# Hymba layer in one Trainium2 core: down products in 3, 4 and 4 pairs, splits in another order, work moved at the stage borders

## The chip, the cores and the metric

One Trainium2 chip, one of its cores. The metric is the device time of one execution of the whole kernel in microseconds (us), lower is better. Five engines work beside each other, each with a queue of its own: TensorE (PE, matmuls; its weight loads are shown as PEld), ScalarE (ACT), VectorE (DVE), GpSimd (POOL) and SyncE (SP, which here issues DMAs).

## The reference

One layer on 512 tokens, with 16 meta tokens put in front (L = 528 columns), width 1024, FFN width 2816, all float32:

```python
h = jnp.concatenate([meta, x], axis=1)
h = h + 0.5 * swiglu_ffn(rms_norm(h, ffn1_norm), ffn1_w_gu, ffn1_w_down)
h = h + hybrid_mixer(rms_norm(h, mix_norm), w_in, conv_w, b_f, ...)   # short conv + attention with forget gates
h = h + 0.5 * swiglu_ffn(rms_norm(h, ffn2_norm), ffn2_w_gu, ffn2_w_down)
return rms_norm(h[:, 16:], final_norm)

def swiglu_ffn(h, w_gu, w_down):
    gate, up = jnp.split(h @ w_gu, 2, axis=-1)
    return (jax.nn.silu(gate) * up) @ w_down
```

## The kernel before

**Layout.** The activations lie transposed: features on the 128 partitions, tokens along the free dimension. The residual stream `hT` has 8 tiles of 128 features. A weight is the stationary operand of a matmul, the activations move past it. Float32 accuracy comes from a split: an operand is cut into a part `hi` (rounded, by a cast on ACT) and a part `lo` (the rest, by a subtraction on DVE), and a product is three matmuls, hi·hi, hi·lo and lo·hi.

**Stages.** FFN1 (528 tokens, in two halves of 264 columns), the mixer, FFN2 (512 tokens, halves of 256), the final norm. At the start of each FFN some gate and up tiles are computed one by one ("classical", with splits on lines L450 and L454), while the forms of the normed input are made. FFN1 splits its last classical weights behind the norm.

**Units.** All else in the FFNs is done in *units*. A unit multiplies a 2x2 block arrangement (two output tiles by two token halves) by a scheme with seven products in place of eight. `gates(f)` and `ups(f)` make two tiles of gate or up over 4 pairs of input tiles; `down(j0, nj, m)` adds `nj` pairs of hidden tiles into two tiles of `hT`. A unit has seven *slots* of 3·nj matmuls each on PE (L522), in this order: p1 (weights `nat`), p4 of the unit before (its weights `s1`), p2 (`nat`), p6 (`s24`), p5 (`s1`), p7 (`s3`), pC (`s24`). p2 may start only when ACT has copied bank B = −A (L535), p7 only after C = −B (L536). A slot of 12 matmuls takes about 1.5 us.

**The weights of a unit** are made in `prep`: SP loads the raw block, two POOL DMAs (L478) add to it in place, DVE makes the sums s2 and s4 (L481, L484), and then each of `nat`, `s24`, `s1`, `s3` is split: `hi` on ACT (L492), one slot later `lo` on DVE (L496). The moving operands are *forms*, which `pair_forms` makes for each pair of tiles (sums on POOL, L379 to L382, hi on ACT, L368, lo on DVE, L369), and they lie in a ring in an arena.

**Order.** Everything is written into numbered slots: `sl.at(t, fn, prio)` puts an instruction beside slot t; within a slot lower `prio` stands first. Results have 0, forms 2, `prep` 3. The engines work through their queues in that order. So a DVE instruction that waits (for the end of a product, say) holds up all that stands behind it on DVE. The results of a unit at slot b on DVE are, for ups: b+3 `times(0,0)`, b+6 `c22` (L581 and L577), b+7 `c12` (L585 and L577), b+9 `times(1,0)` (L577), which reads the bank that p4 ended one slot before; for downs the adds into `hT` (L604, L607, L608) at the same places.

**FFN1's downs** are done in four rounds of 3, 3, 2 and 3 pairs, each of 4 units; in the last round `fin` makes the mixer's operand (L275, L280) and the squares (L289 on ACT, L290 on POOL) for each tile of `hT` as it is done.

Of the kernel before, what the change touches and what calls it, by code (L numbers as in the profile page):

```python
# [14 lines left out]
P = 128  # L15
# [148 lines left out]
def layer(ctx, tc, x, meta, n1, gu1, dn1, nm, w_in, conv_w, b_f, g_conv, g_attn, w_out, n2, gu2, dn2, nf, out):  # L164
# [174 lines left out]
    class Ffn:  # L339
# [31 lines left out]
        def pair_forms(self, r, s0, s1, t0, t1, soon=True):  # L371

            h, ts = self.h, {}
            d, e = (0, 3) if soon else (1, 4)

            def sums():
                t = ts["t"] = self.pool.tile([P, 4, h], F32, name="ts")
                b11, b12, b21, b22 = (self.half(s(), i) for s in (s0, s1) for i in range(2))
                nc.gpsimd.tensor_sub(t[:, 0], b11, b12)  # L379
                nc.gpsimd.tensor_add(t[:, 1], t[:, 0], b22)  # L380
                nc.gpsimd.tensor_sub(t[:, 2], b12, b22)
                nc.gpsimd.tensor_sub(t[:, 3], b21, t[:, 1])  # L382

            self.split_forms(r, F_B11, F_B11 + 1, lambda: self.half(s0(), 0), t0 + d)
            self.sl.at(t1, sums)
            self.split_forms(r, F_B21, F_B22 + 1, lambda: s1()[:, :2 * h].rearrange("p (a c) -> p a c", a=2), t1 + d)
            self.split_forms(r, F_T1, F_T4 + 1, lambda: ts["t"], t1 + e)

        def x_pair(self, j, t):
# [11 lines left out]
            self.pair_forms(self.xform(j), lambda: xs[0], lambda: xs[1], t + 1, t + 1)  # L401

        def hidden_pair(self, j, t0, t1, soon=False):
            self.pair_forms(self.hform(j), lambda: self.hd[2 * j], lambda: self.hd[2 * j + 1], t0, t1, soon)
# [55 lines left out]
        def prep(self, b, mat, c0, j0, nj):  # L460
# [47 lines left out]
        def products(self, nj, rhs, w):  # L508
# [86 lines left out]
        def down(self, j0, nj, m):  # L595
# [3 lines left out]
            b, q, A, B, C, E = self.products(nj, lambda j: self.hform(j0 + j), w)  # L599
# [17 lines left out]

    with tc.tile_pool(name="ps1", bufs=3, space=PSUM) as ps1, tc.tile_pool(name="ps1s", bufs=2, space=PSUM) as ps1s:
# [5 lines left out]
        with tc.tile_pool(name="xin", bufs=1) as xin:  # L624
# [50 lines left out]
            with tc.manual_schedule(engines={mybir.EngineType.PE, mybir.EngineType.Activation, mybir.EngineType.DVE}):  # L675
# [29 lines left out]
                for j in range(3):  # L705
                    t = t528("raw")
                    accs[j].each(lambda ps, g: nc.scalar.copy(g(t), ps))
                    raws_f.append(t)
                h, lo = split2(ssum, L)
                a3, _ = new1()  # L710
                mm(a3, W.take(3), range(4), xh, xl, last=False)
                sms = [ps1s.tile([P, 512], F32, name="sm") for _ in range(2)]
                sa = Acc(sms, L)
                row_sums(sa, h, lo)
                mm(a3, W.take(3), range(4, ND), xh, xl, first=False)
                row_rstd(sa)
                t = t528("raw")
                a3.each(lambda ps, g: nc.scalar.copy(g(t), ps))
                raws_f.append(t)
            gp = ps1s.tile([P, 512], F32, name="sm")  # L720
            nc.tensor.transpose(gp[:, :36], gt, ident[:36, :36])
            nc.vector.tensor_copy(gains[:, 8:], gp[:, :36])
            nc.vector.tensor_scalar(ghalf, gains[:, :24], -0.5, None, ALU.mult)
# [13 lines left out]
    with tc.tile_pool(name="ffn1", bufs=1, reuse_waits="tile") as pool, tc.manual_schedule(engines=ENGINES):  # L737
# [4 lines left out]
        ring = lambda j: 0 if j == 10 else RING + (j + 3) % 4 * 14 * 264  # L742
# [60 lines left out]
    with ExitStack() as mix:  # L803
# [459 lines left out]
```

## Time and profile before

| | |
|---|---|
| median of 3 runs | 1000.1 us (998.0 to 1001.9) |
| the profiled execution | 1000.34 us, its span 998.6 us, so 1.7 us lie around the span |
| PE busy | 951.8 us, 95% of the span |
| DVE, ACT, POOL busy | 780.3 us (78%), 586.1 us (59%), 350.9 us (35%) |
| mean granted clock of TensorE | 0.988 of full |

Busy time of PE includes matmuls at the lower clock, so idle time is not all that PE loses. In rows of the trace "idle before <-X" names what ended the idle time; "128x1024" is partitions by elements.

### The profile page before, as it was taken

To read this page: it belongs to the slowest core of one execution; us is meant where nothing else is said; L and a number is where in the kernel's file an instruction comes from. 1 tells how busy PE (TensorE), PEld (TensorE's weight loads), DVE (VectorE), ACT (ScalarE), POOL (GpSimd) and SP (SyncE) were. 2 spreads that over 40 slices of the span, in tenths; PEclk is the share of its full clock that TensorE was granted. 3 is DMA by queue.
4 is the path that set the end of the run, shared out by engine and by line. 5 is a ranking of instruction groups with operands and counts; after the bars stand their busy time and mean duration, and the time that the engine had idled before them with its cause. 6 is when DMAs were issued, how large, how long until landed. Compare 5 with 4: busy or idle time off the path is not lost.

```text
span 998.6 us, 17874 instructions
## 1 busy us (share of the span) xinstructions
PE 951.8 (95%) x7022; PEld 907.8 (91%) x7022; DVE 780.3 (78%) x1260; ACT 586.1 (59%) x1044; POOL 350.9 (35%) x323
## 2 busy tenths in 40 slices
PE   9898999999999998999999999999999999999995
PEld 8798999999999887989899888778999999999984
DVE  5688887888788887786767657788897988788655
ACT  5544655665666564785656565545655665576444
POOL 4247533553444564100000000365533653444302
PEclk9999999999999999999999999999999999999997
DMA  6236488668784571542222221257589668787612
GB/s 193 64 107 138 100 174 181 134 128 183 164 156 100 116 141 45 130 107 64 64 78 65 77 64 43 79 137 163 108 171 188 133 132 183 172 153 170 130 29 85
DMA packets 176261, 121.01 MB, mean 121 GB/s; under 512 B 5845, under 2 KB 175617, under 8 KB 176177
## 3 DMA queue, kind: packets, MB, share of 16 engines
q1 hardware_dynamic: 117024, 90.42, 29.9%
q0 software_dynamic: 59008, 28.93, 23.8%
q8 instruction: 55, 0.90, 0.4%
q10 hardware_dynamic: 144, 0.52, 0.1%
q14 instruction: 30, 0.24, 0.1%
HBM read 117.69 MB, written 2.10 MB: 120 GB/s over the span
## 4 chain that ended last, share of the span: by engine, by line
PE 73%; DVE 16%; ACT 5%; issue 4%; POOL 1%; DMA 1%; SPq 0%; ACTq 0%; DVEq 0%
PE bank L522 47%; PE bank L318 19%; DVE w_lo L496 4%; DVE arena L369 3%; PE bank L1055 2%; DVE hT L604 1%; DVE w_lo L454 1%; DVE w_lo L81 1%; PE bank L992 1%; PE bank L1022 1%; ACT arena L275 1%; DVE xn L398 1%; PE acc L318 1%; DVE arena L280 1%; ACT w_hi L492 1%
## 5 line engine op out<-in xcount | busy, mean ns | idle before, releaser
L522 PE MATMUL bank<-arena,w_hi 128*128 128x256 f32 (+1 forms) x3080 | 569.4, 287 | 17.5 <-ACT bank L536 10.0
L522 PEld LDWEIGHTS bank<-arena,w_hi 128*128 128x128 f32 x3080 | 481.7, 191 | 24.1 <-ACT bank L536 14.0
L522 PE MATMUL bank<-arena,w_lo 128*128 128x264 f32 (+1 forms) x1540 | 439.4, 285 | 4.5 <-DVE w_lo L496 4.5
L522 PEld LDWEIGHTS bank<-arena,w_lo 128*128 128x128 f32 x1540 | 294.8, 191 | 6.1 <-DVE w_lo L496 5.9
L318 PE MATMUL bank<-arena,w_hi 128*128 128x264 f32 (+2 forms) x1152 | 247.3, 323 | 3.1 <-ACT w_hi L450 3.1
L492 ACT CAST w_hi<-raw 128x1024 fp32r<-128x1024 f32 (+2 forms) x186 | 176.4, 948 | 125.0 <-DVE raw L484 104.2
L496 DVE TENSOR_TENSOR w_lo<-raw,w_hi 128x1024 fp32r<-128x1024 f32 (+2 forms) x186 | 222.9, 1199 | 31.9 <-ACT w_hi L492 30.2
L318 PEld LDWEIGHTS bank<-arena,w_hi 128*128 128x128 f32 x1152 | 179.6, 191 | 18.9 <-ACT w_hi L450 3.5
L318 PE MATMUL bank<-arena,w_lo 128*128 128x264 f32 (+2 forms) x576 | 155.5, 325 | 5.4 <-DVE w_lo L454 5.3
L318 PEld LDWEIGHTS bank<-arena,w_lo 128*128 128x128 f32 x576 | 96.8, 191 | 15.9 <-DVE w_lo L454 8.4
L478 POOL DMA_DIRECT2D s<-in_ffn_w_gu_dram x34 | 49.7, 1462 | 67.9 <-ACT bank L536 65.9
L81 DVE TENSOR_TENSOR w_lo<-raw,w_hi 128x1024 fp32r<-128x1024 f32 (+2 forms) x53 | 55.3, 1052 | 21.0 <-ACT w_hi L80 20.8
L478 POOL DMA_DIRECT2D raw<-in_ffn_w_gu_dram x34 | 44.1, 1298 | 77.2 <-DMA raw<-in_ffn_w_gu_dram 76.7
L80 ACT CAST w_hi<-raw 128x1024 fp32r<-128x1024 f32 (+3 forms) x54 | 44.1, 829 | 45.2 <-PE bank L318 35.6
L478 POOL DMA_DIRECT2D s<-in_ffn_w_down_dram x28 | 41.2, 1471 | 70.8 <-ACT bank L536 67.3
L604 DVE TENSOR_TENSOR hT<-bank,hT 128x264 f32<-128x264 f32 (+1 forms) x112 | 47.5, 424 | 14.5 <-PE bank L522 14.1
L496 DVE TENSOR_TENSOR w_lo<-s,w_hi 128x512 fp32r<-128x512 f32 (+2 forms) x62 | 46.8, 755 | 0.0
L193 ACT ACTIVATE s<-s 128x256 f32<-128x256 f32 (+3 forms) x42 | 19.4, 461 | 46.5 <-DVE s L561 26.6
L474 ACT COPY s<-raw 128x512 f32<-128x512 f32 (+2 forms) x62 | 35.5, 572 | 17.6 <-DVE w_lo L496 15.2
L369 DVE TENSOR_TENSOR arena<-ts,arena 128x1056 fp32r<-128x1056 f32 (+1 forms) x29 | 35.9, 1237 | 9.4 <-ACT arena L368 9.4
L481 DVE TENSOR_TENSOR raw<-raw 128x512 f32<-128x512 f32 (+2 forms) x62 | 42.0, 677 | 0.8
L478 POOL DMA_DIRECT2D raw<-in_ffn_w_down_dram x28 | 35.4, 1265 | 15.1 <-DMA raw<-in_ffn_w_down_dram 14.5
(231 smaller groups left out, 1170.9 us busy)
## 6 DMA issues: line engine op xcount, KB each, us to landing
raw<-in_ffn_w_gu_dram SPq DMA_DIRECT2D x34, 1024.0 KB, 6.7
raw<-in_ffn_w_down_dram SPq DMA_DIRECT2D x20, 768.0 KB, 4.4
raw<-in_w_in_dram SPq DMA_DIRECT2D x24, 512.0 KB, 4.1
raw<-in_ffn_w_gu_dram POOLq DMA_DIRECT2D x34, 256.0 KB, 4.8
s<-in_ffn_w_gu_dram POOLq DMA_DIRECT2D x34, 256.0 KB, 6.2
raw<-in_ffn_w_gu_dram SPq DMA_DIRECT2D x16, 512.0 KB, 4.0
raw<-in_ffn_w_down_dram SPq DMA_DIRECT2D x4, 1024.0 KB, 5.1
raw<-in_ffn_w_down_dram POOLq DMA_DIRECT2D x20, 192.0 KB, 4.4
```

The costliest lines, as they stand in the source:

```text
L80: nc.scalar.copy(h, src)
L81: nc.vector.tensor_sub(lw, src, h.bitcast(F32))
L318: nc.tensor.matmul(ap, lhsT=wt[:, kw, :], rhs=mt[:, k, c0 - off:c1 - off], start=(first and a == 0 and b == 0), stop=(last and a == len(ks ...
L369: self.sl.at(t + 1, lambda: nc.vector.tensor_sub(lo, src(), hi.bitcast(F32)), 2)
L474: nc.scalar.copy(raw["s3"], raw["all"][:, 0::2, 0])
L478: nc.gpsimd.dma_start(out=t, in_=mat_j[:, i, :, c0 + P:c0 + 2 * P], accum_op=ALU.add)
L481: nc.vector.tensor_add(raw["all"][:, 0::2, 0], raw["all"][:, 0::2, 1], raw["all"][:, 0::2, 0])
L492: nc.scalar.copy(w[nm_][0][:, :m], src(nm_))
L496: nc.vector.tensor_sub(w[nm_][1][:, :m], src(nm_), w[nm_][0][:, :m].bitcast(F32))
L522: nc.tensor.matmul(bank, lhsT=wt[:, idx(j), :], rhs=r[:, form, part], start=(start and i == 0), stop=(i == last), skip_group_check=True)
L604: return lambda: nc.vector.tensor_add(t, ps, t)
L1055: nc.tensor.matmul(oo, lhsT=lt, rhs=rt, start=(a == 0 and n_ == 0), stop=(a == 1 and n_ == len(ops) - 1))
```

## The change

1. **The order of the splits in every unit.** `prep` splits `s1` at slot b and `s24` at b+1; before it was `s24` at b and `s1` at b+1. `nat` and `s3` stay where they were.
2. **FFN1's downs** go in three rounds of 3, 4 and 4 pairs, at other places between the gates and ups: 28 units in FFN1 in place of 32, with the same number of matmuls. The forms of the last hidden pair are made one by one (`last_pair`), their sums on DVE. In the first unit of the last round p5 stands ahead of p2 and p6 (`late`).
3. **Forms at the FFNs' start.** The pairs of the normed input stand 6 slots apart in place of 5, from slot 8 (FFN1) and 5 (FFN2) in place of 9 and 6; a different part of each pair is split early; two hidden pairs move by one or two slots.
4. **FFN1's start.** The transposes of the gains stand ahead of the norm's sums, and two weights (gate and up of tile 2) are loaded and split ahead of the classical products that use them.
5. **FFN2's end.** The loads of the last two weight rows are issued 12 and 11 slots earlier, and their splits two slots earlier.
6. Some addresses of the mixer's operands in the arena change.

```diff
-        def pair_forms(self, r, s0, s1, t0, t1, soon=True):
+        def pair_forms(self, r, s0, s1, t0, t1, e, d=0):
-            d, e = (0, 3) if soon else (1, 4)
...
-            self.pair_forms(self.xform(j), lambda: xs[0], lambda: xs[1], t + 1, t + 1)
+            self.pair_forms(self.xform(j), lambda: xs[0], lambda: xs[1], t + 1, t + 1, 4)
...
+        def last_pair(self, j, b):
...
+            split(F_B11, 1, lambda: src(0, 0), b + 3)
+            split(F_B22, 1, lambda: src(1, 1), b + 6)
+            sl.at(b + 7, sums, 0)
+            split(F_T1, 3, lambda: v["t"][:, :3], b + 7)
+            sl.at(b + 9, lambda: nc.vector.tensor_sub(v["t"][:, 3], src(1, 0), v["t"][:, 1]), 0)
+            split(F_B21, 1, lambda: src(1, 0), b + 9)
+            split(F_T4, 1, lambda: v["t"][:, 3], b + 9)
...
-            for nm_, t in (("nat", b - 4), ("s24", b), ("s1", b + 1), ("s3", b + 2)):
+            for nm_, t in (("nat", b - 4), ("s1", b), ("s24", b + 1), ("s3", b + 2)):
                 sl.at(t, lambda nm_=nm_: hi(nm_), 3)
                 sl.at(t + 1, lambda nm_=nm_: lo(nm_), 3)
...
+            for p in (p5, p2, p6) if late else (p2, p6, p5):
+                sl.slot(p)
...
+            wts2 = [split_raw2(0)]
             row_rstd(sa)
             table(SILU_SET)
+            out_of(a3)
+            wts2.append(split_raw2(1))
...
-            F.x_pair(j, 9 + 5 * j)
+            F.x_pair(j, 8 + 6 * j)
...
         g_units(range(8, 14))
+        F.gates(14)
         for m in range(0, ND, 2):
-            F.down(3, 3, m)
-        g_units(range(14, NF))
+            F.down(3, 4, m)
+        t = F.ups(14)
+        F.hidden_pair(7, t, t)
+        g_units(range(16, NF - 2))
+        F.gates(NF - 2)
+        F.ups(NF - 2)
+        F.last_pair(NF // 2 - 1, len(sl.pe) - 7)
         for m in range(0, ND, 2):
-            F.down(6, 2, m)
-        for m in range(0, ND, 2):
-            for i, t in enumerate(F.down(8, 3, m)):
+            for i, t in enumerate(F.down(7, 4, m, m == 0)):
...
-                F.x_pair(j, 6 + 5 * j)
-            F.hidden_pair(0, n0 - 5, n0 - 5, True)
-            F.hidden_pair(1, n0 + 1, n0 + 1, True)
+                F.x_pair(j, 5 + 6 * j)
+            F.hidden_pair(0, n0 - 3, n0 - 3, True)
+            F.hidden_pair(1, n0 + 2, n0 + 2, True)
...
-                sl.at(n - 10 + 6 * i, W.load, 4)
-                sl.at(n - 4 + 3 * i, lambda: W.split(False), 4)
+                sl.at(n - 22 + 7 * i, W.load, 4)
+                sl.at(n - 6 + 3 * i, lambda: W.split(False), 4)
```

How this moves instructions in the built programs is shown at three places. **First place:** DVE's queue in a gates unit that follows an ups unit (FFN2), before the change. `w_lo_8803` is the lo part of `s24`, `w_lo_8820` that of `s1`, and the `L577` between them is `times(1,0)` of the ups, which reads the bank of p4:

```order
L577 SCALAR_TENSOR_TENSOR s_8603<-v_8782,s_8603 128x256
L496 TENSOR_TENSOR w_lo_8803<-raw_8538,w_hi_8802 128x1024
L577 SCALAR_TENSOR_TENSOR s_8604<-bank_7071,s_8604 128x256
L496 TENSOR_TENSOR w_lo_8820<-raw_8538,w_hi_8819 128x1024
L496 TENSOR_TENSOR w_lo_8837<-s3_8615,w_hi_8836 128x512
```

The same place in the changed program, where `w_lo_8682` belongs to `s1` and `w_lo_8699` to `s24`:

```order
L604 SCALAR_TENSOR_TENSOR s_8482<-v_8661,s_8482 128x256
L521 TENSOR_TENSOR w_lo_8682<-raw_8417,w_hi_8681 128x1024
L604 SCALAR_TENSOR_TENSOR s_8483<-bank_6950,s_8483 128x256
L521 TENSOR_TENSOR w_lo_8699<-raw_8417,w_hi_8698 128x1024
L521 TENSOR_TENSOR w_lo_8716<-s3_8494,w_hi_8715 128x512
```

The lo part of `s24`, which p6 reads, now stands behind the instruction that waits for p4, where the lo part of `s1` stood, which p5 reads one slot later.

**Second place:** ACT's queue at the start of FFN2, where its classical products begin, before the change; `xn` is the normed input of a pair, `ts` its sums, L450 the hi split of a classical weight:

```order
L193 ACTIVATE s<-s 128x512
L450 CAST w_hi<-raw 128x1024
L368 CAST arena<-xn 128x256
L368 CAST arena<-xn 128x2x256
L368 CAST arena<-ts 128x4x256
L450 CAST w_hi<-raw 128x1024
```

In the changed program (there L475 is the same split):

```order
L193 ACTIVATE s<-s 128x512
L368 CAST arena<-xn 128x256
L368 CAST arena<-xn 128x2x256
L475 CAST w_hi<-raw 128x1024
L368 CAST arena<-ts 128x4x256
L475 CAST w_hi<-raw 128x1024
```

The first two casts of pair 0 now stand ahead of the first weight's split; on DVE their lo parts stand ahead of its lo part in the same way.

**Third place:** DVE's queue in the last round of FFN1's downs, one unit with `fin` (L280), before the change. `w_lo_4341` is the lo part of `s24`, `w_lo_4360` that of `s1`:

```order
L604 TENSOR_TENSOR hT_67<-bank_518,hT_67 128x264
L280 SCALAR_TENSOR_TENSOR arena_70<-hT_67,gains_75,arena_70 128x528
L496 TENSOR_TENSOR w_lo_4341<-raw_4135,w_hi_4340 128x768
L604 TENSOR_TENSOR hT_67<-bank_516,hT_67 128x264
L496 TENSOR_TENSOR w_lo_4360<-raw_4135,w_hi_4359 128x768
```

In the changed program, where `w_lo_4178` belongs to `s1` and `w_lo_4200` to `s24`:

```order
L631 TENSOR_TENSOR hT_67<-bank_533,hT_67 128x264
L280 SCALAR_TENSOR_TENSOR arena_70<-hT_67,gains_75,arena_70 128x528
L521 TENSOR_TENSOR w_lo_4178<-raw_3911,w_hi_4177 128x1024
L631 TENSOR_TENSOR hT_67<-bank_531,hT_67 128x264
L521 TENSOR_TENSOR w_lo_4200<-raw_3911,w_hi_4199 128x1024
```

Again the lo part of `s24` stands one split and one add later; with four pairs each split has 1024 elements in place of 768.

## Rows read from the trace of the kernel before

**Rows 1.** The page: span, and busy time of each engine.

```profile
span 998.6 us, 17874 instructions
PE 951.8 (95%) x7022; PEld 907.8 (91%) x7022; DVE 780.3 (78%) x1260; ACT 586.1 (59%) x1044; POOL 350.9 (35%) x323
```

**Rows 2.** Windows by stage: length; busy PE, PEld, DVE, ACT, POOL; PEclk, DMA, GB/s.

```profile
26.00:104.00 78.00, 69.27 (x513) 67.33 (x513) 60.86 (x80) 38.54 (x62) 37.63 (x33) 0.93 0.43 105
330.00:395.00 65.00, 56.07 (x420) 52.39 (x419) 56.20 (x103) 35.51 (x68) 33.49 (x35) 1.00 0.50 99
692.00:960.00 268.00, 263.67 (x2177) 261.32 (x2176) 220.74 (x325) 159.86 (x273) 112.77 (x87) 1.00 0.72 150
```

**Rows 3.** PE's waits, whole span: us in total, times, longest.

```profile
PE bank L522 <- ACT bank L536: 10.0, 19, 1.2
PE bank L318 <- DVE w_lo L454: 5.3, 8, 1.5
PE bank L522 <- ACT bank L535: 4.8, 3, 2.5
PE bank L522 <- DVE w_lo L496: 4.5, 5, 1.8
```

**Rows 4.** Windows, PE alone: length, busy (matmuls that touch it), PEclk, DMA, GB/s.

```profile
374.00:378.00 4.00, 2.51 (x20) 1.00 0.29 36
...
680.45:683.86 3.41, 3.41 (x18) 0.50 0.09 10
684.20:687.61 3.41, 3.41 (x30) 1.00 0.95 183
```

**Rows 5.** Timeline of one gates unit in FFN1: DVE, ACT, PE (start, duration).

```profile
287.83 1.62 DVE L496 TENSOR_TENSOR w_lo<-raw,w_hi 128x1024 fp32r<-128x1024 f32 x1 [0.37 <-ACT w_hi L492]
289.47 0.43 DVE L577 SCALAR_TENSOR_TENSOR s<-bank,s 128x264 f32<-128x264 f32 x1
289.82 1.33 DVE L496 TENSOR_TENSOR w_lo<-raw,w_hi 128x1024 fp32r<-128x1024 f32 x1
...
288.01 0.38 ACT L535 ACTIVATE bank<-bank 128x264 f32<-128x264 f32 x1 [0.21 <-PE bank L522]
...
290.99 0.28 PE L522 MATMUL bank<-arena,w_lo 128*128 128x264 f32 x1
```

**Rows 6.** Timeline of PE at FFN1's start: the two longest waits.

```profile
40.99 0.75 PE L318 MATMUL bank<-arena,w_hi 128*128 128x264 f32 x4 [2.19 <-ACT w_hi L450]
...
98.82 0.39 PE L522 MATMUL bank<-arena,w_hi 128*128 128x264 f32 x1 [2.46 <-ACT bank L535]
```

**Rows 7.** Timeline at FFN1's end: POOL, DVE, and one of PE's waits.

```profile
373.83 1.30 POOL L290 TENSOR_TENSOR ssum<-ssum,sq 128x528 f32<-128x528 f32 x1 [1.62 <-ACT sq L289]
...
373.87 2.09 DVE L496 TENSOR_TENSOR w_lo<-raw,w_hi 128x768 fp32r<-128x768 f32 x1
376.22 0.94 DVE L496 TENSOR_TENSOR w_lo<-raw,w_hi 128x768 fp32r<-128x768 f32 x1
...
376.01 0.39 PE L522 MATMUL bank<-arena,w_lo 128*128 128x264 f32 x1 [1.49 <-DVE w_lo L496]
```

**Rows 8.** Timeline at FFN2's start: PE's longest waits, and ACT, DVE ahead of them.

```profile
636.52 1.03 ACT L450 CAST w_hi<-raw 128x1024 fp32r<-128x1024 f32 x1
...
638.58 1.76 DVE L454 TENSOR_TENSOR w_lo<-raw,w_hi 128x1024 fp32r<-128x1024 f32 x1
640.87 1.56 DVE L369 TENSOR_TENSOR arena<-xn,arena 128x256 fp32r<-128x256 f32 x2
...
640.39 0.50 PE L318 MATMUL bank<-arena,w_lo 128*128 128x512 f32 x1 [1.51 <-DVE w_lo L454]
679.92 0.38 PE L522 MATMUL bank<-arena,w_hi 128*128 128x256 f32 x1 [2.06 <-ACT bank L535]
```

**Rows 9.** Timeline at FFN2's end: DVE, PE.

```profile
972.35 1.23 DVE L81 TENSOR_TENSOR w_lo<-raw,w_hi 128x1024 fp32r<-128x1024 f32 x1 [5.97 <-ACT w_hi L80]
...
973.96 0.58 PE L522 MATMUL bank<-arena,w_hi 128*128 128x256 f32 x1 [2.06 <-DVE v L581]
```

More of the change, by code (lines that the diff above doesn't have):

```diff
@@ L400, in x_pair, with src, split, sums @@
             self.sl.at(t, norm)
-            self.pair_forms(self.xform(j), lambda: xs[0], lambda: xs[1], t + 1, t + 1)
+            self.pair_forms(self.xform(j), lambda: xs[0], lambda: xs[1], t + 1, t + 1, 4)
         def hidden_pair(self, j, t0, t1, soon=False):
-            self.pair_forms(self.hform(j), lambda: self.hd[2 * j], lambda: self.hd[2 * j + 1], t0, t1, soon)
+            self.pair_forms(self.hform(j), lambda: self.hd[2 * j], lambda: self.hd[2 * j + 1], t0, t1, *((3, 0) if soon else (4, 1)))
+        def last_pair(self, j, b):
+            h, r, sl, v = self.h, self.hform(j), self.sl, {}
+            def src(i, k):
+                return self.half(self.hd[2 * j + i], k)
+            def split(f, n, s, t):
+                hi, lo = (r[:, f:f + n, i] if n > 1 else r[:, f, i] for i in range(2))
+                sl.at(t, lambda: nc.scalar.copy(hi, s()), 0)
+                sl.at(t + (f in (F_B22, F_T1)), lambda: nc.vector.tensor_sub(lo, s(), hi.bitcast(F32)), 0)
+            def sums():
+                t = v["t"] = self.pool.tile([P, 4, h], F32, name="ts")
+                nc.vector.tensor_sub(t[:, 0], src(0, 0), src(0, 1))
+                nc.vector.tensor_add(t[:, 1], t[:, 0], src(1, 1))
+                nc.vector.tensor_sub(t[:, 2], src(0, 1), src(1, 1))
+            split(F_B11, 1, lambda: src(0, 0), b + 3)
[5 more added lines that the diff above has]
+            split(F_T4, 1, lambda: v["t"][:, 3], b + 9)
         def classical(self, f, acc_g, acc_u, xop, wts_=None, hd_pool=None):
@@ L506, in prep, with products @@
             return w
-        def products(self, nj, rhs, w):
+        def products(self, nj, rhs, w, late=False):
             sl, h = self.sl, self.h
@@ L704, in layer @@
                         squares(d + 1, L, nc.gpsimd)
[L705 to L714, printed above, removed]
@@ L715, in layer @@
-                mm(a3, W.take(3), range(4, ND), xh, xl, first=False)
-                row_rstd(sa)
+                gp = ps1s.tile([P, 512], F32, name="sm")
+                nc.tensor.transpose(gp[:, :36], gt, ident[:36, :36])
+                nc.vector.tensor_copy(gains[:, 8:], gp[:, :36])
+                nc.vector.tensor_scalar(ghalf, gains[:, :24], -0.5, None, ALU.mult)
+        pool1 = ffn1.enter_context(tc.tile_pool(name="ffn1", bufs=1, reuse_waits="tile"))
+        raw2 = []
+        for c in (2 * P, DFF + 2 * P):
+            raw2.append(pool1.tile([P, 2048], F32, name="raw", bufs=3)[:, :1024].rearrange("p (k c) -> p k c", c=P))
+            nc.sync.dma_start(out=raw2[-1], in_=gu1.rearrange("(k p) n -> p k n", p=P)[:, :, c:c + P])
@@ L717, in layer, with split_raw2, out_of @@
+        with tc.manual_schedule(engines={mybir.EngineType.PE, mybir.EngineType.Activation, mybir.EngineType.DVE}):
+            def split_raw2(i):
+                w = (wts.tile([P, 8, P], F32R, name="w_hi"), wts.tile([P, 8, P], F32R, name="w_lo"))
+                nc.scalar.copy(w[0], raw2[i])
+                nc.vector.tensor_sub(w[1], raw2[i], w[0].bitcast(F32))
+                return w
+            def out_of(acc):
                 t = t528("raw")
-                a3.each(lambda ps, g: nc.scalar.copy(g(t), ps))
+                acc.each(lambda ps, g: nc.scalar.copy(g(t), ps))
@@ L719, in layer @@
                 raws_f.append(t)
[L720 to L723, printed above, removed]
+            for j in range(3):
+                out_of(accs[j])
+            h, lo = split2(ssum, L)
+            a3, _ = new1()
+            mm(a3, W.take(3), range(4), xh, xl, last=False)
+            sms = [ps1s.tile([P, 512], F32, name="sm") for _ in range(2)]
@@ L724, in layer @@
+            sa = Acc(sms, L)
+            row_sums(sa, h, lo)
+            mm(a3, W.take(3), range(4, ND), xh, xl, first=False)
+            wts2 = [split_raw2(0)]
+            row_rstd(sa)
             table(SILU_SET)
+            out_of(a3)
+            wts2.append(split_raw2(1))
         for _ in range(4):
@@ L735, in new @@
         return Acc([bank() for _ in range(1 if n <= 512 else 2)], n)
-    with tc.tile_pool(name="ffn1", bufs=1, reuse_waits="tile") as pool, tc.manual_schedule(engines=ENGINES):
+    with ffn1, tc.manual_schedule(engines=ENGINES):
+        pool = pool1
         sl = Slots()
@@ L775, in g_units @@
                 t = F.ups(f)
-                F.hidden_pair(f // 2, t, t)
+                F.hidden_pair(f // 2, t, t, soon=f == 12)
         g_units(range(NC1, 8))
```

24 lines of the change are left out of this document (12 added, 12 removed).

## The prediction

> **What bounds the kernel now.** First the page [rows 1]: PE is busy 95% of the span, DVE 78%, ACT 59%. So PE sets the time, and the change leaves PE's work alone: FFN1's downs have 3+3+2+3 = 11 pairs before and 3+4+4 = 11 after, in fewer units. What can change is time in which PE waits or runs slowly. Then the windows by stage [rows 2]: in the long middle of FFN2 PE idles 268.00 − 263.67 = 4.3 us only, while FFN1's start idles 8.7 us in 78 and FFN1's end 8.9 us in 65. These short borders are where something can be gained, and the long stretches are where something can be lost. Then PE's waits [rows 3]: for L536 ahead of p7 10.0 us in 19 waits, for the splits of classical weights 5.3, for L535 ahead of p2 4.8, for the lo parts of a unit's weights (L496) 4.5 in only 5 places. The reader is to keep that last row: today a unit's lo parts are in time nearly everywhere. Last the clock [rows 4]: in 3.41 us at a granted clock of 0.50 (1.2 GHz of 2.4) 18 matmuls touch the window, in as long a stretch at full clock 30. Twelve fewer at 0.1195 us each cost 1.43 us. The trace has five such stretches: two behind waits in FFN1's classical start, three behind the waits of 2.46, 2.06 and 2.06 us in [rows 6, 8, 9]. A wait of 1.49 us, which 374 to 378 holds, was followed by none [rows 4, 7].
>
> The Trainium skill, "TensorE: Matmul & The Clock Gate", Part 1, counts the price of a throttled stretch as its time by (1 − K/N). By it each stretch costs 3.41 · 0.5 = 1.7 us, not 1.43, so the sum below, which has 1.5 fewer such stretches than before, would come out 0.4 us lower.
>
> **The order of the splits, in every unit.** Take the gates unit in [rows 5]. DVE makes the first lo part (287.83 to 289.45), then L577, which waits for p4 and ends at 289.90, then the second lo part (289.82 to 291.15). Before, the first is that of s24 and the second that of s1. PE needs s24's at its first lo matmul of p6, at 290.99, and s1's a whole slot (1.5 us) later, so nothing waits. After the change the queues show s1 first and s24 behind L577. L577 can't move, since p4 ends when it ends. So p6's third matmul finds its operand 291.15 − 290.99 = 0.16 us late; PE starts 0.05 us after such a release (375.96 to 376.01 in [rows 7]) and its first matmul takes 0.39 in place of 0.28 us. That is 0.32 us. Twelve gates units follow an ups unit (6 in each FFN): 12 · 0.33 = 4.0 us. Behind downs, and in downs with four pairs, the second lo part runs undisturbed and lands a little earlier; I take 0.22 us, between 0 and the 0.32 of the row. By the new program these are 17 units: 3.8 us. Ups behind gates have no result to wait for between the two splits, and the first downs behind other units wait for L536 anyway: nothing. Sum **+7.8** (bounds 0, if the second split starts early enough after all, and 29 · 0.35 = 10).
>
> **FFN1's middle.** A round of 3-pair downs after ups has about three of the 19 waits for L536, 0.53 us in the mean and 0.11 for each restart. With four pairs in a round the slots are longer and these go: **−2.0** (0 to −3).
>
> **FFN1's start.** The waits of [rows 6] are 2.19 us at 38.8 for a weight split on ACT behind the norm, a second one at 73, and 2.46 us for L535, which stands behind s24's hi split, which waits for the sum s4. With the other order L535 no longer stands behind it, but s24's hi still waits for s4, and its lo part now has s1's lo part, the last x pair's lo and a first form of the hidden pair ahead of it. At the durations of such rows (1.2 to 1.6 us each) p6 waits about 3.0 us (2 to 4). The two weights split ahead take away the first wait; from the new queues I expect waits of some 0.7, 0.9, 0.75 and 1.4 us in the later classical slots, where x pairs stand ahead of splits. So 6.75 us in place of 7.0 idle and 0.9 of restarts: −1.1; and one slow stretch in place of three: −2.9. **−4.0** (−6.5 to −1).
>
> **FFN1's end.** Before, 65.00 − 56.07 = 8.9 us idle and some 13 restarts, 0.11 us each, and short waits: 11 to 12. In a unit with `fin`, s24's lo takes 2.09 us beside POOL's L290, against 0.94 for the next [rows 7]. After: s1's lo takes this place (2.09, and some 0.27 more for four pairs), then the add (0.35 until the next starts), then s24's lo (1.2): from 373.87 to about 377.8, while p6 with four pairs needs it 6 · 0.1215 = 0.7 us later than at 374.52. A wait of about 2.6 us in two units, some 1.6 in the first, where L290 doesn't collide; 3.5 us in all at the border, where p5 is first and its form waits for the last hidden pair (ACT and DVE one behind the other); 0.8 behind the end. 11.1: **−0.5** (−3 to +2). But waits of 2.6 us are longer than all three that were followed by the lower clock, and 1.49 was not. I take one and a half stretches: **+2.2** (0 to +4.3).
>
> **FFN2's start.** Before, the first weight's hi is cast at 636.52 and its lo made at 638.58 to 640.34; PE waits 1.51 us [rows 8]. After, the casts of pair 0's B parts stand ahead on ACT, and these wait for DVE's normed input (637.26 to 638.67), so the hi starts near 639.3; on DVE the B parts' lo (1.56) stand ahead too. The lo is then ready at 642 to 643 and PE waits 3 to 4 us. Of the later waits some go and some come, p6 of the first unit waits 2.6 us where p2 waited 2.06; one slow stretch stays. **+1.9** (0 to +3.5).
>
> **FFN2's end.** Before, c22 on DVE stands behind L81 (972.35 to 973.58), and the last p4 waits 2.06 us [rows 9]. Earlier loads put this split ahead: −2.06, and its slow stretch −1.43. Against it, L80 now stands ahead of L536 on ACT (+0.9), and the last operand's cast and lo part, which came in time behind a slow p4, are now waited for (+1.4, from 0.42 + 0.62 + 0.69 us of L577, L1184 and L1185 behind p4). **−1.2** (−2.2 to −0.3). The mixer's addresses move no instruction on PE: 0 (±1).
>
> **The sum.** 7.8 − 2.0 − 4.0 − 0.5 + 2.2 + 1.9 − 1.2 = **+4.2**. On the profiled execution (1000.34 us, 0.2 above the median of the runs, 1.7 around its span) that is **1004.5 us**, 0.4% slower. About 0.5%, 5.0 us, is what a measurement of this kernel can tell from no change, so its borders are 995.1 and 1005.1.
>
> **The rivals.** *The clock decides (slower).* Place: FFN1's last downs and FFN2's start. If every new wait above 2 us is followed by a slow stretch, FFN1's end has three (+2.1 against the sum) and FFN2's start one more (+1.4): 1008.0. It decides as soon as one comes more than counted (1005.9). For it: the three waits named. Against it: waits near 1.5 to 1.75 us at FFN1's end had none.
>
> *The split order is free (no change).* If the second lo part starts before L577, or PE's order gives the slack of 0.16 us in another way, the 7.8 us vanish and the rest remains: 996.7. For it: the lateness is a tenth of a slot, and s1's hi needs no s4, so DVE's first split can start some tenths earlier. Against it: L577's start is set by p4's end, and stands between.
>
> *The borders work as they are meant to (faster).* On top of that the waits at FFN1's end stay under those that were followed by a slow stretch (−2.2) and FFN2's start loses its one (−1.4): 993.1. For it: fewer, longer units give each split more time. Against it: DVE's queue at the third place of the order, with two splits and an add ahead of p6.
>
> **How the numbers follow.** Forecast 0.45, with its own range 1001 to 1008; the clock 0.20; free order 0.20; borders as meant 0.10; something else 0.05. Faster: all of the third rival, a quarter of the second, a little else: 0.16. Same: six tenths of the forecast (0.27), three quarters of the second rival (0.15), 0.02: 0.44. Slower: the rest of the forecast (0.18), the clock (0.20), 0.02: 0.40. The range reaches from the second rival's middle to past the clock's: 996 to 1010.
>
> **What would show it.** PE's waits for w_lo of a unit (L496, then L521) grow from 5 to some 30, near 0.2 us each, in p6. The wait for L535 at FFN1's start goes and one for w_lo of about 3 us takes its place; the idle time at 38.8 and the slow stretch behind it go. FFN1's end has waits of 2.6 us in p6 beside L290, FFN2's start one of 3 to 4 us. The last p4 starts without a wait for c22. Wrong would be: w_lo waits in fewer than ten units (then about 997), or more than four slow stretches (then past 1005).

## The result, and the profile after

The changed kernel takes 1007.8 us (median of 4 runs, 1006.7 to 1008.7); the kernel before 999.8 us (median of 4 runs). The ratio is 1.0079, 95% interval 1.0055 to 1.0102: slower by 0.8%, past the 0.5% that the prediction took for no change. The profiled execution took 1007.0 us. Its page, as in [rows 1], has the same 7022 matmuls and a span 6.7 us longer:

```profile
span 1005.3 us, 17767 instructions
PE 955.9 (95%) x7022; PEld 909.3 (90%) x7022; DVE 770.1 (77%) x1218; ACT 582.9 (58%) x1018; POOL 339.6 (34%) x311
```

PE's waits over the span (us in total, times, longest), to be read against [rows 3]; L562 and L563 are L535 and L536 of before, L521 is L496, L479 is L454:

```profile
PE bank L547 <- DVE w_lo L521: 11.9, 11, 2.6
PE bank L547 <- ACT bank L563: 4.9, 8, 1.0
PE bank L547 <- ACT bank L562: 4.4, 2, 4.0
PE bank L318 <- DVE w_lo L479: 4.1, 5, 1.3
PE bank L318 <- ACT w_hi L475: 1.9, 1, 1.9
```

The waits for C = −B fell from 10.0 to 4.9 us, those for a unit's lo parts rose from 4.5 to 11.9 us. Another 29 matmuls with a lo part start 0.1 to 0.25 us late and are not among these 11: matmuls overlap in the trace (they start 0.12 us apart and last 0.28), so that hardly a gap is shown there; they are seen in the starts of the matmuls. The windows by stage, as in [rows 2], with FFN2's start in the third:

```profile
26.00:104.00 78.00, 71.27 (x554) 69.40 (x553) 65.46 (x86) 42.40 (x68) 44.39 (x38) 0.98 0.46 114
330.00:395.00 65.00, 55.45 (x400) 52.82 (x400) 49.51 (x73) 32.37 (x52) 23.85 (x29) 0.95 0.40 85
640.00:692.00 52.00, 46.25 (x210) 39.14 (x211) 41.66 (x47) 24.40 (x37) 33.93 (x28) 0.87 0.56 137
692.00:960.00 268.00, 262.66 (x2151) 258.69 (x2150) 215.19 (x320) 160.46 (x273) 111.56 (x87) 1.00 0.72 149
```

Windows at fixed times hold other work in another kernel. So here is the time between five marks that both traces have: the start of L535 in FFN1's second unit, the first matmul on `vs` in the mixer (its L922, L969 after), the start of L535 in FFN2's second unit and in its last, and the end of the span.

| stretch | before | after | difference | forecast |
|---|---|---|---|---|
| start to FFN1's second unit | 109.43 | 104.65 | −4.78 | −4.0 |
| to the mixer's first `vs` | 318.30 | 321.73 | +3.43 | +3.3 |
| to FFN2's second unit | 263.09 | 267.83 | +4.74 | +1.9 |
| to FFN2's last unit | 271.63 | 275.95 | +4.32 | +4.2 |
| to the end | 36.19 | 35.11 | −1.08 | −1.2 |

(Of the forecast's 7.8 us for the split order, FFN2's 6 gates and 10 other units make 6 · 0.33 + 10 · 0.22 = 4.2, FFN1's the other 3.6; with −2.0, −0.5 and +2.2 the second row has 3.3.)

**A gates unit** of FFN1 in the timeline, the place of [rows 5]: DVE, ACT, PE.

```profile
293.85 1.22 DVE L521 TENSOR_TENSOR w_lo<-raw,w_hi 128x1024 fp32r<-128x1024 f32 x1
295.94 0.43 DVE L604 SCALAR_TENSOR_TENSOR s<-bank,s 128x264 f32<-128x264 f32 x1 [0.87 <-PE bank L547]
296.29 1.32 DVE L521 TENSOR_TENSOR w_lo<-raw,w_hi 128x1024 fp32r<-128x1024 f32 x1
...
294.49 0.38 ACT L562 ACTIVATE bank<-bank 128x264 f32<-128x264 f32 x1 [2.00 <-PE bank L547]
294.77 1.04 ACT L517 CAST w_hi<-raw 128x1024 fp32r<-128x1024 f32 x1
...
297.22 0.41 PE L547 MATMUL bank<-arena,w_hi 128*128 128x264 f32 x2
297.67 0.39 PE L547 MATMUL bank<-arena,w_lo 128*128 128x264 f32 x1
```

The lo part of s1 is early (295.07), that of s24 ends at 297.61, and p6's first lo matmul starts at 297.67 in place of 297.46, two steps of 0.12 us after 297.22. The next matmul starts 0.11 us later than usual behind it, so together that is 0.32 us, as worked out. The reader may note two more things: DVE stood idle for 0.87 us ahead of L604, and ACT made s24's hi only at 294.77 to 295.81.

**FFN1's end**, the place of [rows 7], timeline of POOL, DVE, PE:

```profile
365.13 1.34 POOL L290 TENSOR_TENSOR ssum<-ssum,sq 128x528 f32<-128x528 f32 x1 [5.02 <-ACT sq L289]
...
365.17 2.38 DVE L521 TENSOR_TENSOR w_lo<-raw,w_hi 128x1024 fp32r<-128x1024 f32 x1
...
367.81 1.21 DVE L521 TENSOR_TENSOR w_lo<-raw,w_hi 128x1024 fp32r<-128x1024 f32 x1
...
369.08 0.39 PE L547 MATMUL bank<-arena,w_lo 128*128 128x264 f32 x1 [2.51 <-DVE w_lo L521]
```

A split beside POOL's L290 takes 2.38 us in place of 1.21, and it is now s1's, with s24's behind it: p6 waits 2.51 us. In the units before and behind this one p6 waits 1.35 and 0.89 us; the forecast had 1.6 us once and 2.6 us twice. The Trainium skill, "SBUF — State Buffer", section "SBUF: two separate sides", says that a DVE instruction with two SBUF inputs and a GpSimd instruction that reads SBUF exclude each other for a whole instruction; the trace agrees, since the split is longer by 1.17 us beside an L290 of 1.34.

Two stretches at the lower clock, called slow stretches from here on, fall here. The first begins behind the wait of 2.51 us. Ahead of the second PE waits twice, for less than 1 us each; the rows are PE's timeline, then windows of PE as in [rows 4]:

```profile
381.96 0.73 PE L318 MATMUL bank<-arena,w_hi 128*128 128x512 f32 x2 [0.87 <-ACT w_hi L80]
383.58 0.39 PE L547 MATMUL bank<-arena,w_lo 128*128 128x264 f32 x1 [0.89 <-DVE w_lo L521]
...
370.36:373.77 3.41, 3.41 (x18) 0.50 0.13 7
384.01:387.42 3.41, 3.41 (x18) 0.50 0.59 154
```

**FFN2's start**, the place of [rows 8], timeline of PE's waits, then POOL and ACT ahead of the last:

```profile
638.92 0.73 PE L318 MATMUL bank<-arena,w_hi 128*128 128x512 f32 x2 [1.89 <-ACT w_hi L475]
640.99 0.80 PE L318 MATMUL bank<-arena,w_lo 128*128 128x512 f32 x1 [1.34 <-DVE w_lo L479]
682.60 0.80 PE L547 MATMUL bank<-arena,w_hi 128*128 128x256 f32 x2 [3.96 <-ACT bank L562]
...
675.45 1.65 POOL L378 TENSOR_TENSOR ts<-hd 128x256 f32<-128x256 f32 x1 [4.67 <-DVE arena L369]
...
679.07 1.18 POOL L381 TENSOR_TENSOR ts<-hd,ts 128x256 f32<-128x256 f32 x1
...
680.29 1.04 ACT L368 CAST arena<-ts 128x1024 fp32r<-128x1024 f32 x1 [3.88 <-POOL ts L381]
681.24 1.04 ACT L517 CAST w_hi<-raw 128x1024 fp32r<-128x1024 f32 x1
682.18 0.36 ACT L562 ACTIVATE bank<-bank 128x256 f32<-128x256 f32 x1
```

The first weight waits as forecast (1.89 and 1.34 us, together 3.2). But p2 of the first unit waits 3.96 us for L562, and this stands on ACT behind the cast of hidden pair 0's sums, which POOL begins late (L378, the first of these sums, after 4.67 us without work) and ends at 680.25. And the windows of PE at the lower clock (length, busy, matmuls that touch it, PEclk, DMA, GB/s), as in [rows 4], are twice as long as any of before:

```profile
640.01:646.84 6.83, 5.85 (x14) 0.50 0.34 97
680.97:687.80 6.83, 5.20 (x24) 0.50 0.78 121
```

### The profile page after: what moved, and what is told of

Same layout as the page of the kernel before. It is cut to its first block, busy times and chain, and to the rows that moved or that the text cites. A ratio compares the mean times of both kernels' runs of the same rounds, so it can differ in the third digit from the quotient of the medians.

```text
span 1005.3 us, 17767 instructions
## 1 busy us (share of the span) xinstructions
PE 955.9 (95%) x7022; PEld 909.3 (90%) x7022; DVE 770.1 (77%) x1218; ACT 582.9 (58%) x1018; POOL 339.6 (34%) x311
## 4 chain that ended last, share of the span: by engine, by line
PE 51%; DVE 10%; ACT 4%; issue 2%; DVEq 0%; ACTq 0%
PE bank L547 27%; PE bank L318 18%; DVE w_lo L521 3%; PE bank L1102 2%; PE bank L1039 1%; PE bank L1069 1%; DVE arena L369 1%; ACT arena L275 1%; DVE hT L631 1%; ACT w_hi L517 1%; DVE w_lo L81 0%; DVE arena L280 0%; PE bank L910 0%; DVE ssum L290 0%; PE bank L1210 0%
## 5 line engine op out<-in xcount | busy, mean ns | idle before, releaser
L547 PE MATMUL bank<-arena,w_lo 128*128 128x264 f32 (+1 forms) x1540 | 444.0, 288 | 13.1 <-DVE w_lo L521 11.9
L521 DVE TENSOR_TENSOR w_lo<-raw,w_hi 128x1024 fp32r<-128x1024 f32 (+1 forms) x174 | 214.2, 1231 | 16.5 <-ACT w_hi L517 14.8
L517 ACT CAST w_hi<-raw 128x1024 fp32r<-128x1024 f32 (+1 forms) x174 | 173.8, 999 | 66.4 <-PE bank L547 66.4
L81 DVE TENSOR_TENSOR w_lo<-raw,w_hi 128x1024 fp32r<-128x1024 f32 (+2 forms) x53 | 55.9, 1065 | 18.2 <-ACT w_hi L80 17.7
L562 ACT ACTIVATE bank<-bank 128x256 f32<-128x256 f32 (+1 forms) x58 | 21.5, 371 | 72.0 <-PE bank L547 72.0
L631 DVE TENSOR_TENSOR hT<-bank,hT 128x264 f32<-128x264 f32 (+1 forms) x96 | 40.7, 424 | 28.3 <-PE bank L547 26.9
L503 POOL DMA_DIRECT2D s<-in_ffn_w_down_dram x24 | 34.5, 1436 | 76.5 <-ACT bank L563 76.5
L521 DVE TENSOR_TENSOR w_lo<-s,w_hi 128x512 fp32r<-128x512 f32 (+1 forms) x58 | 47.4, 817 | 0.0
L499 ACT COPY s<-raw 128x512 f32<-128x512 f32 (+1 forms) x58 | 34.7, 598 | 16.7 <-DVE w_lo L521 12.6
L506 DVE TENSOR_TENSOR raw<-raw 128x512 f32<-128x512 f32 (+1 forms) x58 | 40.1, 691 | 0.8
L378 POOL TENSOR_TENSOR ts<-s 128x256 f32<-128x256 f32 (+1 forms) x15 | 23.1, 1541 | 52.0 <-DVE s L604 52.0
```

The costliest lines, as they stand in the source:

```text
L81: nc.vector.tensor_sub(lw, src, h.bitcast(F32))
L499: nc.scalar.copy(raw["s3"], raw["all"][:, 0::2, 0])
L503: nc.gpsimd.dma_start(out=t, in_=mat_j[:, i, :, c0 + P:c0 + 2 * P], accum_op=ALU.add)
L506: nc.vector.tensor_add(raw["all"][:, 0::2, 0], raw["all"][:, 0::2, 1], raw["all"][:, 0::2, 0])
L517: nc.scalar.copy(w[nm_][0][:, :m], src(nm_))
L521: nc.vector.tensor_sub(w[nm_][1][:, :m], src(nm_), w[nm_][0][:, :m].bitcast(F32))
```

## The experiments

Each is compared with runs of the kernel before on the same chip. The twelve ran on three chips, four on each, so across these the ratios are compared, not the times. The first four take the two large losses apart.

**s24 first again.** In the changed kernel, with the new order kept in the one unit that takes p5 first:

```diff
-            for nm_, t in (("nat", b - 4), ("s1", b), ("s24", b + 1), ("s3", b + 2)):
+            two = ("s1", "s24") if s1_first else ("s24", "s1")
+            for nm_, t in (("nat", b - 4), (two[0], b), (two[1], b + 1), ("s3", b + 2)):
...
```

> The changed kernel (1007.8 us) with s24 split ahead of s1 again in every unit but the one that takes p5 first. Theory (the lo part of s24 comes too late for p6): FFN2's middle gets back the 4.3 us that its 29 units lost in the trace, FFN1's middle about 3, and FFN1's last downs 1 to 4 by shorter waits beside L290: 997 to 1000, and the waits of PE for a unit's w_lo fall from 11 counted ones and some 20 short ones to fewer than 8. Rival (the loss sits at the stage borders, the order of splits is free): 1006 to 1009.

Measured: 996.2 us, 0.9968 of before (0.9955 to 0.9980), a little under the range of the theory. The order of two splits costs some 11 us of the changed kernel (11.1 by the ratios, 11.6 by the medians), and the rest of the change is a gain of 0.3%. PE's waits for C = −B in FFN1, between its second unit and the mixer, first in the kernel before, then here (L564 is L536), then in the changed kernel (us in total, times, longest):

```profile
PE bank L522 <- ACT bank L536: 5.9, 11, 1.2
PE bank L548 <- ACT bank L564: 5.1, 6, 2.3
PE bank L547 <- ACT bank L563: 2.0, 4, 0.8
```

So the longer rounds alone take 0.8 us of these waits. Most of the fall in the changed kernel is the order's: where p6 waits first, p7 finds C in time.

**Only the new order in the kernel before** (the same line, the other way).

> The kernel before (999.8 us) with the new order of splits and nothing else of the change. Theory: 7 to 10 us slower, 1007 to 1010, with waits for w_lo of 0.2 to 0.35 us in p6 of nearly every unit but ups behind gates. Rival (order free): 999 to 1001.

Measured: 1013.2 us, 1.0139 (1.0116 to 1.0162): more than expected. FFN1's stretch alone loses 7.2 us (table below), with a slow stretch of 6.83 us in it.

**FFN2's start as before, in the changed kernel.** The added 3 is the number of slots from a pair's sums to their splits; the changed kernel has 4 for these pairs.

```diff
-                F.x_pair(j, 5 + 6 * j)
-            F.hidden_pair(0, n0 - 3, n0 - 3, True)
-            F.hidden_pair(1, n0 + 2, n0 + 2, True)
+                F.x_pair(j, 6 + 5 * j, 3)
+            F.hidden_pair(0, n0 - 5, n0 - 5, True)
+            F.hidden_pair(1, n0 + 1, n0 + 1, True)
...
```

> The changed kernel with the slots of the forms at FFN2's start (pairs of the normed input and the first two hidden pairs) as they were before, the order of splits as changed. Theory (the casts of pair 0 ahead of the first weight, and hidden pair 0 ahead of L535, cost 4.8 us there, slow stretches included): 1002 to 1004, with at most one slow stretch between 635 and 690. Rival (the waits only move to other slots): 1006 to 1008.

Measured: 1005.8 us, 1.0061 (1.0041 to 1.0081). The expectation failed, by 2 us, and the time lies just under the rival's range: with s1 first, p6 of FFN2's first unit waits 2.7 us for a lo part, and a slow stretch of 6.83 us is still there.

**Both undone.**

> The changed kernel with both undone: s24 ahead of s1 and FFN2's start as before; left are the 3, 4 and 4 pairs, FFN1's start and FFN2's end. Theory (the two losses add up, the rest of the change gains): 993 to 996, faster than the kernel before. Rival (the remaining parts give nothing on balance): 999 to 1001.

Measured: 991.7 us, 0.9921 (0.9900 to 0.9942), faster than the theory's range. Together the two losses are all of it: what is left of the change is 0.8% faster than before. In the stretch to FFN2's second unit they overlap: it is 267.8 us with both, 268.1 and 265.7 with one undone, and 263.0 with none. In the whole times an overlap does not stand out from the noise. The stretches between the marks, from the profiled executions:

| kernel | FFN1 start | to mixer | to FFN2's 2nd unit | to its last | to the end |
|---|---|---|---|---|---|
| before | 109.4 | 318.3 | 263.1 | 271.6 | 36.2 |
| changed | 104.6 | 321.7 | 267.8 | 275.9 | 35.1 |
| s24 first again | 102.1 | 316.7 | 268.1 | 271.4 | 34.9 |
| before, s1 first | 107.2 | 325.5 | 266.6 | 276.0 | 35.4 |
| FFN2's start as before | 105.4 | 321.8 | 265.7 | 276.1 | 35.1 |
| both undone | 102.7 | 317.9 | 263.0 | 271.6 | 34.9 |

FFN2's long stretch is 275.9 to 276.1 in all three kernels with s1 first and 271.4 to 271.6 in the others: here nothing but the order counts, and it is worth 4.4 to 4.5 us.

**Why s24's lo part is late.** In the kernel before with s1 first, only the DVE instruction with p4's result is put behind the second split:

```diff
-            sl.at(b + 9, lambda: times(1, 0, B), 0)
+            sl.at(b + 9, lambda: times(1, 0, B), 4)
...
-            sl.at(b + 9, add(h10, B), 0)
+            sl.at(b + 9, add(h10, B), 4)
```

> The kernel before with the new order of splits, as run above (1013.2 us), and one thing more: the DVE instruction with p4's result stands behind the second split in place of ahead of it. Theory (s24's lo is late only because it is queued behind the instruction that waits for p4): the 271.6 us between FFN2's second and last unit come back (276.0 without this), FFN1's steady units too, and only its last downs and FFN2's start stay slower: 1002 to 1006. Rival (the order itself costs, on ACT or by s1 being split before s24 on DVE): 1010 to 1014.

Measured: 1013.6 us, 1.0113 (1.0096 to 1.0131). The expectation failed. FFN2's long stretch came back only half, to 273.8; the first stretch had slow clock again (109.4), and FFN1's grew to 326.4, perhaps because the adds that `fin` waits for came later (argued from the queue, not tested). The half that came back is the downs': FFN2's last three units, 0.23 us longer each with s1 first, take as long as before here. The gates units keep their loss, and one of them shows why: the timeline of DVE, POOL and PE.

```profile
784.33 1.22 DVE L496 TENSOR_TENSOR w_lo<-raw,w_hi 128x1024 fp32r<-128x1024 f32 x1
786.28 1.76 DVE L496 TENSOR_TENSOR w_lo<-raw,w_hi 128x1024 fp32r<-128x1024 f32 x1 [0.74 <-ACT w_hi L492]
787.97 0.41 DVE L577 SCALAR_TENSOR_TENSOR s<-bank,s 128x256 f32<-128x256 f32 x1
...
786.93 1.72 POOL L381 TENSOR_TENSOR ts<-s 128x256 f32<-128x256 f32 x1
...
788.10 0.39 PE L522 MATMUL bank<-arena,w_lo 128*128 128x256 f32 x1
```

The split no longer stands behind L577, but it waits for its hi part on ACT until 786.26, then runs beside POOL's sums and takes 1.76 in place of 1.22 us: 788.04, p6 as late as before. In the gates units two limits lie on the same spot, and taking one away uncovers the other.

**Both splits a slot earlier, s1 still first.** On the kernel with both losses undone:

```diff
-            for nm_, t in (("nat", b - 4), (two[0], b), (two[1], b + 1), ("s3", b + 2)):
+            for nm_, t in (("nat", b - 4), ("s1", b - 1), ("s24", b), ("s3", b + 2)):
```

> The kernel with both losses undone (991.7 us), but s1 split one slot earlier than in the changed kernel (b - 1) and s24 at slot b: s1 still first, and both lo parts ahead of p4's result on DVE. Theory (what counts is where the split stands against the instruction that waits for p4, not which is first): the stretch between FFN2's second and last unit stays at 271.4 to 272.2 and the whole at 990 to 992, less if FFN1's last downs gain. Rival (s1 first costs in itself): 996 or more.

Measured: 985.7 us, 0.9840 (0.9821 to 0.9859), the fastest of all, and below what was expected. FFN2's long stretch is 270.6, FFN1's 312.4. Of the 5.5 us that FFN1's lost against the kernel with both undone, 2.9 are two slow stretches that are gone, and PE's waits fell from 10.1 to 7.3 us. Its waits of PE and the windows by stage:

```profile
PE bank L547 <- ACT bank L563: 7.5, 10, 1.7
PE bank L547 <- DVE w_lo L521: 6.1, 8, 1.3
```

```profile
330.00:395.00 65.00, 59.49 (x447) 56.19 (x446) 53.04 (x76) 37.24 (x60) 22.46 (x28) 1.00 0.45 94
692.00:960.00 268.00, 263.79 (x2177) 261.36 (x2177) 213.97 (x321) 161.01 (x271) 104.56 (x82) 1.00 0.69 145
```

No wait for a lo part is over 1.3 us now, FFN1's end idles 5.5 us in place of 9.6, and no stretch at the lower clock is left ahead of the last 8 us, in which PE is done.

**The same edit alone, in the changed kernel and in the one before.**

> The changed kernel with one edit: s1 split at slot b - 1 and s24 at b in place of b and b + 1. Theory (the 11.6 us between the changed kernel and the one with the old order are the lateness of s24's second split): all of it comes back and some more at FFN1's last downs; left is the loss at FFN2's start, 2 to 5 us against the kernel run above at 0.984 of before: 0.986 to 0.990 of before. Rival (half of the loss is the order itself or the waits that moved): 0.995 or more.

Measured: 990.3 us, 0.9903 (0.9886 to 0.9920): 17.6 us less than the changed kernel by the ratios, all of the 11 us of the order and more; the theory's range is met but for 0.0003.

> The kernel before with s1 split at b - 1 and s24 at b, nothing else. Theory (also before, the second lo part and the last downs' splits came close to their use): the stretch between FFN2's second and last unit falls from 271.6 to 270.7, FFN1's last downs wait less for p6: 0.993 to 0.997 of before. Rival (before nothing waited for these splits, so nothing is gained): 0.999 to 1.001.

Measured: 999.8 us, 1.0004 (0.9992 to 1.0016). The rival holds: 1.0 us is gained in FFN2's long stretch (270.6) and lost again between FFN1's second unit and the mixer (321.1), where p7 of a `fin` unit waits longer and two slow stretches fall.

**With both early, FFN1's downs as before** (3, 3, 2 and 3 pairs with their places, addresses and forms).

> The kernel run above at 0.984 of before (both splits early, FFN2's start as before) with FFN1's downs in 3, 3, 2 and 3 pairs again, with their places, addresses and the last pair's forms as before. Theory (3, 4 and 4 pairs give little: FFN1's stretch was 317.9 with them and 318.3 without): 0.983 to 0.987. Rival (fewer, longer units give 4 us once the splits are in time): 0.988 to 0.990.

Measured: 993.8 us, 0.9939 (0.9923 to 0.9955). The expectation failed: the new rounds are worth 0.9840 against 0.9939, some 10 us by the ratios and 6.8 us in the stretch of FFN1 (319.2 against 312.4). Of the 6.8, PE's waits are 4.1 (11.4 against 7.3) and one slow stretch 1.4; the rest was not taken apart. With s24 first the new rounds seemed to give 0.4 us only (318.3 against 317.9), because the kernel with both undone had two slow stretches there and the kernel before none.

**What FFN2's start waits for.** In the kernel with s24 first again, hidden pair 0 back at its slot (`n0 - 5`):

> The first of the four kernels above (s24 first, 996.2 us) with hidden pair 0 of FFN2 back two slots, the pairs of the normed input left as changed. Theory (the hi cast of this pair's sums, which waits for four POOL sums, stands ahead of L535 and makes p2 wait 4.0 us): that wait falls to about 2 us and the stretch from the mixer's end to FFN2's second unit loses 2 to 3.5 of the 5.0 us: 993 to 994. Rival (the casts of pair 0 ahead of the first weight cost it all): 995.5 to 997.

Measured: 996.3 us, 0.9951 (0.9933 to 0.9969), the stretch 268.6. The expectation failed; the wait for L535's successor grew from 4.0 to 5.4 us. The timeline of POOL, ACT, DVE, PE in this kernel (its L563 is L535):

```profile
665.14 1.65 POOL L378 TENSOR_TENSOR ts<-hd 128x256 f32<-128x256 f32 x1 [4.38 <-DVE arena L369]
...
669.34 1.04 ACT L368 CAST arena<-ts 128x1024 fp32r<-128x1024 f32 x1 [4.07 <-POOL ts L381]
...
671.56 0.68 DVE L509 TENSOR_TENSOR raw<-raw 128x512 f32<-128x512 f32 x1
...
673.72 0.80 PE L548 MATMUL bank<-arena,w_hi 128*128 128x256 f32 x2 [5.38 <-ACT bank L563]
```

POOL had nothing to do for 4.38 us: it waited until DVE had read the sums (`ts`) of the last pair of the normed input. So two slots earlier did not bring the sums of the hidden pair forward, and behind them come s4 (L509), the hi split and L535's successor. That points at the pairs of the normed input, 6 apart:

```diff
-                F.x_pair(j, 5 + 6 * j)
+                F.x_pair(j, 6 + 5 * j, 3)
...
```

> The kernel with s24 first (0.9968 of before in the first call) with FFN2's pairs of the normed input 5 slots apart from slot 6 again, the hidden pairs as changed. Theory (the last of these pairs comes two slots later and hands on its one buffer of sums later, so hidden pair 0's sums on POOL and with them s4, s24's hi and L535 come late; pair 0's casts hold up the first weight): both waits fall to those before, and the stretch from the mixer to FFN2's second unit from 268.1 to 263 to 264 us: 0.991 to 0.993 of before. Rival (hidden pair 0's own slot makes the wait of 4.0 us): 266 or more, 0.995.

Measured: 993.2 us, 0.9937 (0.9920 to 0.9953), the stretch 264.6, against 263.0 with all slots as before: just past the theory's range, and nearer to it than to the rival's. 3.4 of the 5.0 us are these pairs, 1.6 the hidden pairs' slots. p2 waits 1.2 us in place of 4.0, but p7 of the same unit now waits 2.6, so that PE's waits in this stretch fall only from 8.7 to 8.1 us; the rest goes with the lower clock, of which this profiled execution has 6.83 us less there. The ratios, over all runs, differ by 3.1 us as well.

**p5 not first.** In the kernel with both undone, `F.down(7, 4, m)` for all four. In this order p2 stands ahead of the making of the last pair's B21 form that it reads, so it takes old contents of the ring and waits for nothing: it is the time of a kernel without that wait.

> The kernel with both losses undone (991.7 us), with p5 of the first of the last downs in its usual place and s24 first there too. Theory (p5 first hides part of the wait for the last pair's forms): 1 to 3 us slower, 993 to 995. Rival (this unit's order does not matter, since the other forms come as late): 991 to 992.5.

Measured: 990.2 us, 0.9886 (0.9869 to 0.9904). It is under both ranges and tells nothing on the order: FFN1's stretch is 314.7 against 317.9, and two slow stretches of 1.4 us each that the other had are 2.9 of these 3.2.

## Why the prediction was right, and where not

**The whole: inside the range, and the forecast 3.3 us low.** 1007.8 lies in 996 to 1010, but the loss is 8.0 us by the medians and 6.6 by the five stretches where 4.2 was forecast; of the difference in these, FFN2's start is 2.8 us over its term and the other four stretches together 0.4 under theirs. The prediction's own sign of being wrong, more than four slow stretches and a time past 1005, came: five from 97 us on, two of them of double length, and one more before 12 us.

**The order of splits: right in size, half right in cause.** FFN2's long stretch, where nothing else changed, lost 4.32 us (4.2 forecast), and the kernels with and without the order differ by 4.4 to 4.5. The lateness in p6 and its 0.32 us are in the trace as worked out. But the sentence that L577 in front of the second split makes it late names, in the gates units, only one of two limits: with L577 behind it, the hi part on ACT and POOL's sums beside it gave the same lateness. What the runs show is plainer: with s24's split one slot earlier, and s1 still first, the loss is gone. Its price in the whole kernel is some 11 us, or 14 in the kernel before (by the ratios). That is more than the term of 7.8, and not to be set against it alone: the order also lengthens waits at the borders, which the prediction has in its terms for FFN1's start and end.

**FFN1's start: right** (−4.78 against −4.0), by the mechanism forecast: the wait of 2.19 us is gone, and p6 waits for a lo part instead, 2.58 us against 3.0. 2.9 of the 4.0 forecast were two slow stretches fewer. They came, but that part is less sure than it looks: the kernel before with s1 first has the same classical start, and none there.

**FFN1's middle and end: right in the sum, in part by luck** (+3.43 against +3.3). There is a wait of 2.5 us in p6 of a `fin` unit (2.6 forecast), but once and not twice. Two slow stretches came where one and a half were taken, but one of them behind waits of 0.87 and 0.89 us, not behind one over 2 us. The −2.0 for the waits for C = −B is not borne out as a gain of the four-pair rounds: with s24 first again these waits fall by 0.8 us and five restarts. The experiments show that the new rounds are a gain, which the order of splits hid.

**FFN2's end: right** (−1.08 against −1.2). The last p4 no longer waits for c22, and PE waits 1.5 us for the last operand's cast (L1231) instead, as in the sum.

**FFN2's start: the step that was mis-sized**, +4.74 against +1.9, outside its own 0 to 3.5. The waits ahead of the first weight were right (3.2 us, 3 to 4 forecast). Two things were missed. The text had p2's wait for L535 replaced by one of 2.6 us in p6 (which is there, 2.7 us, only with FFN2's start as before); in fact p2 waited 3.96 us, because the last pair of the normed input comes two slots later and holds the buffer that the next sums need. And "one slow stretch stays" was wrong: two stretches of 6.83 us came, as long as four of before. The waits in this stretch grew by about 1.9 us (1.89 + 1.34 + 0.70 + 3.96 against 6.0). In the slow stretches PE was busy for 11.05 us, which at 1.43 us for 3.41 cost an estimated 4.6 us against 1.4 before: 1.9 + 3.2 = 5.1, for the 4.74 measured. So the clock is the larger part of the miss.

The median of 1007.8 is nearer to the 1008.0 of the rival in which the clock decides than to the forecast. That rival was priced at the right place in FFN2, though by another wait, and with three slow stretches at FFN1's end where two came. The rival with a free order is excluded by the first two experiments. The borders did not work as they were meant to; FFN1's does in the kernel at 0.984, once the splits are in time, and FFN2's start had to be taken back there.

## What to carry to other kernels

When an operand's making moves by one slot, look at every engine on which it is made: here ACT's cast, DVE's place behind a result, and POOL's work beside it all ended at the same moment, and removing one of them gave half of it in the quiet stretch, none of it in the gates units and nothing clear of the noise in the whole. A gain can hide behind a loss in the same diff: the change as a whole was 0.8% slower, and with one line of it moved by a slot and three others taken back it is 1.6% faster than before. A buffer of which there is one (the sums of a pair) turns a shift of its first user into a wait of the second, and here moving the second two slots ahead did not help.

## What the runs showed of the hardware

The same wait was followed by the lower clock in one execution and not in another. In the kernel before with s1 first, FFN1's start has the first wait of [rows 6]; first the timeline of PE, then the windows of PE alone (length, busy, PEclk, DMA, GB/s):

```profile
41.04 0.75 PE L318 MATMUL bank<-arena,w_hi 128*128 128x264 f32 x4 [2.19 <-ACT w_hi L450]
```

```profile
40.00:48.00 8.00, 6.45 (x50) 1.00 0.23 66
74.00:82.00 8.00, 7.27 (x60) 1.00 0.45 93
```

The kernel before has the same instructions here, and in the same windows:

```profile
40.00:48.00 8.00, 6.50 (x39) 0.79 0.23 66
74.00:82.00 8.00, 7.15 (x44) 0.79 0.36 81
```

So a slow stretch behind a wait of about 2 us is not to be counted as certain. Four kernels share this start; in their first 90 us the kernel before had two slow stretches, with s1 first none, with p4's result put behind as well three (one of them before 12 us), and with both splits early one. It is probably also a part of why one profile can be off the median by 2 us, and of why the first stretch of the table moves between kernels that are equal there.

FFN2's start shows the same. The changed kernel with both splits early has the changed kernel's three long waits there: 1.89, 1.35 and 3.95 us for 1.89, 1.34 and 3.96. Behind the first two came no slow stretch, behind the third one of 3.41 us in place of 6.83, as PE's timeline and window show:

```profile
630.54 0.50 PE L318 MATMUL bank<-arena,w_lo 128*128 128x512 f32 x1 [1.35 <-DVE w_lo L479]
...
669.41 0.79 PE L547 MATMUL bank<-arena,w_hi 128*128 128x256 f32 x2 [3.95 <-ACT bank L562]
...
669.23:672.64 3.41, 3.23 (x15) 0.50 1.15 142
```

Its stretch to FFN2's second unit is 265.4 us against 267.8. What made the difference no run here shows. And a stretch at 1.2 GHz may last 6.83 us as well as 3.41.
